# An MLP up-projection as seven half-size products for each pair of weight tiles, with the weight sums on GpSimd and the down-projection interleaved

## The chip, the cores and the metric

The kernel runs on one core of a Trainium2 chip. TensorE (PE in the profile) multiplies matrices into PSUM, VectorE (DVE), ScalarE (ACT) and GpSimd (POOL) work elementwise, and SyncE (SP) issues most DMAs. The metric is the device time of one execution in microseconds (us); lower is better.

## The reference, cut to what matters

One layer of a hybrid diffusion block works on 512 latent tokens and 256 context tokens of width 1024. The change touches only its last part, the MLP:

```
def sq_relu_mlp(h, w1, w2):
    a = jax.nn.relu(h @ w1)
    return (a * a) @ w2

x = x + g2 * sq_relu_mlp(modulate(rmsnorm(x, norm2_g), sh2, sc2), mlp_w1, mlp_w2)
return rmsnorm(x, final_g)
```

`h` is 512 x 1024, `w1` is 1024 x 4096, `w2` is 4096 x 1024, all in float32.

## The kernel before

**Precision.** Every float32 operand is split into a high part in the format float32r and a low part (the rest). `split` does this with an ACT cast (L58) and a DVE subtraction (L59). A product is three matmuls, high by high, high by low and low by high (`mm3`, L71 to L73). `weights` fetches a 128 x 1024 weight tile by DMA into the pool `wraw` (2 buffers), and splits it into the pool `wsp` (3 buffers).

**The MLP.** `h` is kept transposed in `h2`. The 4096 hidden columns are 32 weight tiles of 128. `up` makes for each tile 8 x 3 = 24 matmuls of 512 columns into one PSUM bank, then `square_relu` reads the bank and writes a hidden tile `aT` (high and low). After each 8 tiles, `down` takes the 8 hidden tiles of the chunk before through `w2`, in 2 x 4 steps of 24 matmuls of 512 columns (bank tiles `pd`, stationary `aT`, moving weights), and adds the result to `y2` (the tile `acc`).

**The turn into the MLP.** `half1(t)` makes the second half of the output projection for the token tile t (0 to 3) and from it `xn`, the normalized rows; the factor of the norm comes from a small GpSimd power (L93, tile `ss`). `norm2(t, xn)` transposes `xn` on PE and splits it into `h2`. The first three up tiles are made in halves of 256 columns, so that PE can work on the tokens 0 to 255 while the tokens 256 to 511 are still being normalized.

**Order.** A scheduler lays down one order for each engine when the program is built; each engine takes its instructions strictly in that order, and waits at the first that isn't ready. Where a pool has no free buffer, the first writer of the next tile waits for the last reader of the old one.

Of the kernel before, what the change touches and what calls it, by code (L numbers as in the profile page):

```python
# [36 lines left out]
def dit_block(ctx: ExitStack, tc: tile.TileContext, a: dict):  # L37
# [31 lines left out]
    def mm3(out, st, mv, start, stop):

        PE.matmul(out, st[0], mv[0], start=start, stop=False)  # L71
        PE.matmul(out, st[0], mv[1], start=False, stop=False)  # L72
        PE.matmul(out, st[1], mv[0], start=False, stop=stop)  # L73
# [559 lines left out]
    def hidden():
        return zp[len(aTs) % 2].tile([P, 2, 8, SEQ], F32R, tag="aT", name="aT")

    def up_part(pu, w, lo, n):
        for k in range(KD):
            mm3(pu[:, lo:lo + n], [w[:, h, k * P:(k + 1) * P] for h in range(2)],
                [h2[:, h, k, lo:lo + n] for h in range(2)], k == 0, k == KD - 1)

    def square_relu(pu, aT, i):
        r = sgp.tile([P, SEQ], F32, tag="sg", name="r")
        S.activation(r, pu, AF.Relu)  # L643
        V.tensor_tensor(r, r, r, op=ALU.mult)  # L644
        split(aT[:, 0, i, :], aT[:, 1, i, :], r)

    def up(c, aT, i0=0):
        for i in range(i0, 8):
            w = weights(a["w1"][c * 8 + i])
            pu = psZ.tile([P, 512], F32, tag="u", name="pu1")  # L650
            up_part(pu, w, 0, SEQ)
            square_relu(pu, aT, i)

    def down(c, aT):
        for n in range(2):
            sl = slice(n * 512, (n + 1) * 512)
            pd = [psZ.tile([P, 512], F32, tag="d", name="pd") for _ in range(NT)]
            for ii in range(4):
                w = weights(a["w2"][c, n, ii])
                for t in range(NT):  # L660
                    for i2 in range(2):
                        i = 2 * ii + i2
                        mm3(pd[t], [aT[:, h, i, t * P:(t + 1) * P] for h in range(2)],
                            [w[:, h, i2 * 512:(i2 + 1) * 512] for h in range(2)], i == 0, i == 7)
# [22 lines left out]
    aTs = []  # L687
    aTs.append(hidden())
    first = []
    for i in range(3):  # L690
        w = weights(a["w1"][i])
        pu = psZ.tile([P, 512], F32, tag="u", name="pu1")
        first.append((pu, w))
        if i == 0:
            norm2(2, xn2)
        if i == 2:
            norm2(3, xn3)
        up_part(pu, w, 0, 256)
    for i, (pu, w) in enumerate(first):
        up_part(pu, w, 256, 256)  # L700
        square_relu(pu, aTs[0], i)
    go.close()
    zp.append(pool(gz, "zp1", 1, side="right"))
    up(0, aTs[0], 3)
    for c in range(1, 4):
        aTs.append(hidden())
        up(c, aTs[c])
        down(c - 1, aTs[c - 1])
# [126 lines left out]
```

## Time and profile before

| | |
|---|---|
| Time, median of 3 runs | 821.05 us (819.18 to 821.83) |
| The profiled execution's own time | 821.07 us |
| Its span (first to last instruction) | 819.3 us |
| PE, DVE, ACT, POOL busy | 97%, 56%, 38%, 5% of the span |
| Chain of work that ended last | 93% PE |

Busy time counts an instruction from its start to its end. Matmuls overlap in the pipeline, so the rate of PE is read from the distance between starts (the pitch) and not from the duration of one; the same holds, in a smaller measure, for DVE.

### The profile page before, as it was taken

The page shows a single profiled execution, that of the slowest core. Times are in us where ns is not written, and L with a number is a line of the kernel's source. Part 1 is how long each engine was busy: PE and PEld are TensorE (multiplying, and loading weights), DVE is VectorE, ACT ScalarE, POOL GpSimd, SP SyncE. Part 2 cuts the span into 40 slices and gives each one's busy share as a digit, 9 for nine tenths or more (in the row PEclk, how much of TensorE's full clock was granted, in tenths as well). Part 3 has the DMA queues.
Part 4 walks back from the last instruction along what each step waited for, and adds up shares of the span by engine and source line. Part 5 has one row for each costly group of instructions (what it writes and reads, how often), then busy time and mean ns, then how long its engine had stood idle before and what let it go on. Part 6 is the DMA issues. An engine that isn't in the chain of part 4 may idle for free.

```text
span 819.3 us, 10030 instructions
## 1 busy us (share of the span) xinstructions
PE 797.6 (97%) x3944; PEld 659.6 (81%) x3944; DVE 459.8 (56%) x689; ACT 307.6 (38%) x490; POOL 37.8 (5%) x72
## 2 busy tenths in 40 slices
PE   5999998999999999999999999999999999999996
PEld 4779987888877888888888988888888888888885
DVE  4564537797878888434458654442234324433773
ACT  5434436464772322322344244333333222431132
POOL 1000012121210000000000000000000000000001
PEclk9999999999999999999999999999999999999998
DMA  8653232332208887332434032322232233223122
GB/s 331 252 194 106 83 97 62 92 94 78 81 27 313 297 319 251 103 103 97 184 131 154 1 117 90 102 100 82 102 103 83 97 103 102 79 103 103 60 94 103
DMA packets 33522, 103.98 MB, mean 127 GB/s; under 512 B 8002, under 2 KB 8130, under 8 KB 33474
## 3 DMA queue, kind: packets, MB, share of 16 engines
q1 hardware_dynamic: 32834, 100.99, 35.7%
q0 software_dynamic: 640, 2.36, 1.4%
q8 instruction: 31, 0.51, 0.3%
q14 instruction: 17, 0.13, 0.0%
HBM read 98.87 MB, written 2.10 MB: 123 GB/s over the span
## 4 chain that ended last, share of the span: by engine, by line
PE 93%; DVE 3%; ACT 1%; issue 1%; DMA 1%; SPq 0%; POOLq 0%; POOL 0%; DVEq 0%; ACTq 0%
PE pu L73 8%; PE pu L72 8%; PE pu L71 7%; PE pd L71 7%; PE pd L73 7%; PE pd L72 7%; PE pg L73 5%; PE pg L72 5%; PE pg L71 5%; PE pbr L73 2%; PE pbr L72 2%; PE pbr L71 2%; PE vacc L71 2%; PE vacc L72 1%; PE tp L405 1%; PE vacc L73 1%
## 5 line engine op out<-in xcount | busy, mean ns | idle before, releaser
L59 DVE TENSOR_TENSOR w<-raw,w 128x1024 fp32r<-128x1024 f32 x114 | 141.1, 1238 | 132.0 <-ACT w L58 132.0
L58 ACT CAST w<-raw 128x1024 fp32r<-128x1024 f32 x114 | 119.3, 1046 | 158.1 <-PE pd L73 88.3
L73 PE MATMUL pu<-h,w 128*128 128x512 f32 (+1 forms) x280 | 105.6, 377 | 0.0
L72 PE MATMUL pu<-h,w 128*128 128x512 f32 (+1 forms) x280 | 105.4, 376 | 0.0
L71 PE MATMUL pu<-h,w 128*128 128x512 f32 (+1 forms) x280 | 104.0, 371 | 0.0
L71 PE MATMUL pd<-w,aT 128*128 128x512 f32 x224 | 88.0, 393 | 0.0
L73 PE MATMUL pd<-w,aT 128*128 128x512 f32 x224 | 87.6, 391 | 0.0
L72 PE MATMUL pd<-w,aT 128*128 128x512 f32 x224 | 86.9, 388 | 0.0
L73 PE MATMUL pg<-hx,w 128*128 128x512 f32 x192 | 76.4, 398 | 0.0
L72 PE MATMUL pg<-hx,w 128*128 128x512 f32 x192 | 76.2, 397 | 0.0
L71 PE MATMUL pg<-hx,w 128*128 128x512 f32 x192 | 74.9, 390 | 0.0
L644 DVE TENSOR_TENSOR r<-r 128x512 f32<-128x512 f32 x32 | 22.2, 693 | 87.7 <-ACT r L643 87.5
L71 PEld LDWEIGHTS pu<-h,w 128*128 128x128 f32 x280 | 53.6, 191 | 10.1
L72 PEld LDWEIGHTS pu<-h,w 128*128 128x128 f32 x280 | 52.6, 188 | 9.9
L643 ACT ACTIVATE r<-pu 128x512 f32<-128x512 f32 x32 | 19.1, 597 | 109.8 <-PE pu L73 109.8
L73 PEld LDWEIGHTS pu<-h,w 128*128 128x128 f32 x280 | 52.6, 188 | 9.1
L73 PEld LDWEIGHTS pd<-w,aT 128*128 128x128 f32 x224 | 41.9, 187 | 9.9
L72 PEld LDWEIGHTS pd<-w,aT 128*128 128x128 f32 x224 | 42.0, 188 | 9.3
L71 PEld LDWEIGHTS pd<-w,aT 128*128 128x128 f32 x224 | 42.1, 188 | 8.7
L496 DVE SCALAR_TENSOR_TENSOR acc<-ada,sig,acc 128x1024 f32<-128x1024 f32 x32 | 40.9, 1282 | 9.0 <-DMA ada<-in_adaB 8.8
L71 PEld LDWEIGHTS pg<-hx,w 128*128 128x128 f32 x192 | 36.8, 192 | 8.0
L72 PEld LDWEIGHTS pg<-hx,w 128*128 128x128 f32 x192 | 36.1, 188 | 7.9
(258 smaller groups left out, 1445.2 us busy)
## 6 DMA issues: line engine op xcount, KB each, us to landing
raw<-in_w SPq DMA_DIRECT2D x64, 512.0 KB, 3.3
ada<-in_adaB SPq DMA_DIRECT2D x32, 512.0 KB, 4.9
raw<-in_wG SPq DMA_DIRECT2D x24, 512.0 KB, 3.4
raw<-in_adaA SPq DMA_DIRECT2D x16, 512.0 KB, 5.8
raw<-in_wM SPq DMA_DIRECT2D x8, 512.0 KB, 3.3
raw<-in_wO SPq DMA_DIRECT2D x8, 512.0 KB, 3.2
raw<-in_wC SPq DMA_DIRECT2D x6, 512.0 KB, 3.3
q<-q POOLq DMA_DIRECT2D x8, 288.0 KB, 3.1
```

What stands on the lines that cost most here:

```text
L58: S.copy(hi, src)
L59: V.tensor_tensor(lo, src, f(hi), op=ALU.subtract)
L71: PE.matmul(out, st[0], mv[0], start=start, stop=False)
L72: PE.matmul(out, st[0], mv[1], start=False, stop=False)
L73: PE.matmul(out, st[1], mv[0], start=False, stop=stop)
L405: PE.transpose(tp[:, i, :], pr[:, i * P:(i + 1) * P], ident)
L496: V.scalar_tensor_tensor(acc[:, q, :], raw, sigv[:, k, 0:1], acc[:, q, :], op0=ALU.mult, op1=ALU.add)
L643: S.activation(r, pu, AF.Relu)
L644: V.tensor_tensor(r, r, r, op=ALU.mult)
```

## The change

Two hidden tiles form a pair, and the up-projection of a pair is made as a 2 x 2 block product: `h` is cut into four blocks (tokens 0 to 255 and 256 to 511, features 0 to 511 and 512 to 1023), the two weight tiles `ra` and `rb` into their upper and lower 512 features. Strassen's scheme in Winograd's form gives the four blocks of the result with seven products of half-size blocks in place of eight. So a pair takes 7 x 4 x 3 = 84 matmuls of 256 columns in place of 48 of 512.

The blocks of `h` that the products need are `A11`, `A12`, `A22` and four sums (`Sq`), made once in `norm2_first` and `norm2_second`. For the weights of each pair four sums of 512 columns are made on GpSimd (`sums`: `ta` and `tb`). Each pair splits 3.5 tiles (`ra`, `ta`, `tb` and half of `rb`) where it split 2. The results are put together by accumulating in PSUM (bank `A` goes through products 1, 6, 7 and 4) and by copies and adds of 256 columns. Two steps of the down-projection of the chunk before stand inside each pair from pair 4 on. `g1b`, `fgb` and the pools of the stage are placed anew.

```diff
+    A11, A12, A22 = [h2p.tile([P, 2, 4, HT], F32R, name=f"A{q}") for q in ("11", "12", "22")]
...
+    def norm2_first(t, xn):
+        sl = slice(t * P, (t + 1) * P)
+        for g, tp in enumerate(turned(t, xn)):
+            q = (A11, A12)[g]
+            split(q[:, 0, :, sl], q[:, 1, :, sl], tp)
+            (S.copy if g else V.tensor_copy)(Af[:, g, :, sl], tp)
+    def norm2_second(t, xn, Sq):
...
+        a21 = piece("a21")
+        S.copy(a21, t21)
+        s1 = piece("s1")
+        V.tensor_tensor(s1, t22, a21, op=ALU.subtract)
+        keep(0, s1)
+        split(A22[:, 0, :, sl], A22[:, 1, :, sl], t22)
+        s2 = piece("s2")
+        V.scalar_tensor_tensor(s2, s1, -1.0, Af[:, 0, :, sl], op0=ALU.mult, op1=ALU.subtract)
+        keep(1, s2)
+        s3 = piece("s3")
+        V.tensor_tensor(s3, Af[:, 0, :, sl], a21, op=ALU.subtract)
+        keep(2, s3)
+        s4 = piece("s4")
+        V.scalar_tensor_tensor(s4, s2, -1.0, Af[:, 1, :, sl], op0=ALU.mult, op1=ALU.subtract)
+        keep(3, s4)
...
+        def first_weights(self):
+            self.ra = wraw.tile([P, RAW], F32, tag="raw", name="ra")[:, :D]
+            nc.sync.dma_start(self.ra, a["w1"][2 * self.j])
+            self.rb = mx.tile([P, D], F32, tag="rb", name="rb", bufs=2)
+            nc.sync.dma_start(self.rb, a["w1"][2 * self.j + 1])
+            self.w1 = wsp.tile([P, 2, RAW], F32R, tag="w", name="w")
+            split(self.w1[:, 0, :D], self.w1[:, 1, :D], self.ra)
+        def sums(self):
...
+            G.tensor_tensor(ta[:, :512], ra[:, :512], rb[:, :512], op=ALU.add)
+            G.tensor_tensor(ta[:, 512:], ta[:, :512], rb[:, 512:], op=ALU.add)
+            G.tensor_tensor(tb[:, :512], rb[:, :512], rb[:, 512:], op=ALU.add)
+            G.tensor_tensor(tb[:, 512:], ta[:, 512:], ra[:, 512:], op=ALU.add)
...
+            split(self.w2[:, 0, :D], self.w2[:, 1, :D], ta)
+            self.b22 = mx.tile([P, 2, 512], F32R, tag="b22", name="b22")
+            split(self.b22[:, 0], self.b22[:, 1], rb[:, 512:])
...
+        def p7(self):
+            self.product(self.A, self.w3, 0, self.sq(2), False)
+            V.tensor_tensor(self.r[1][:, HT:], self.A[:, :HT], self.a5, op=ALU.add)
+            self.finish(1)
+        def p4(self):
+            self.product(self.A, self.w3, 512, [A22[:, h] for h in range(2)], False)
+            S.copy(self.r[0][:, HT:], self.A[:, :HT])
+            self.finish(0)
...
+    for j, p in enumerate(pairs):
...
+        if j > 1:
+            p.first_weights()
+            p.p1()
+        p.sums()
+        p.p5()
+        if j:
+            pairs[j - 1].p4()
+        if j > 1:
+            p.p2()
+        step(d)
+        p.p6()
+        p.last_sums()
+        p.p3()
+        step(d + 1)
+        p.p7()
+    pairs[15].p4()
```

**What moves on GpSimd, at the turn into the MLP.** These are POOL's instructions there, first of the kernel before: the four powers (`ss`, one for each token tile) stand together.

```order
L490 MEMSET acc 128x4096
L93 TENSOR_TENSOR ss_3555<-ss_3555,mhalf 128x1 x4
L737 TENSOR_TENSOR ss_6036<-ss_6036,mhalf 128x1
```

And of the change (`ta` and `tb` are the weight sums of pair 0, then of pair 1):

```order
L94 TENSOR_TENSOR ss_3559<-ss_3559,mhalf 128x1 x3
L700 TENSOR_TENSOR ta<-ra,rb 128x512
L702 TENSOR_TENSOR tb<-rb 128x512
L701 TENSOR_TENSOR ta<-ta,rb 128x512
L94 TENSOR_TENSOR ss_3559<-ss_3559,mhalf 128x1
L703 TENSOR_TENSOR tb<-ta,ra 128x512
L700 TENSOR_TENSOR ta<-ra,rb 128x512
```

The power of the last token tile now stands behind three weight sums. The first of them needs `rb`, whose buffer lies in memory that `mT` held, so its DMA waits for a matmul six before the end of `half1(3)`.

**What moves on DVE, right behind that power.** In the kernel before, DVE's last rows for the norm are these (xn is the last token tile, h its split; two more h splits follow, and then the hidden tiles begin):

```order
L92 TENSOR_SCALAR ss_3555<-ss_3555 128x1
L59 TENSOR_TENSOR h_3541<-tp_3891,h_3541 128x4x128
L613 SCALAR_TENSOR_TENSOR xn<-xn,ss_3555,b2b 128x512 x2
L59 TENSOR_TENSOR h_3541<-tp_3898,h_3541 128x4x128
```

In the change the last xn is followed by the rest of token tile 2 and then by tile 3 (s_4053 to s_4067 are its four sums, Sq the splits of the sums, w the splits of the weights):

```order
L616 SCALAR_TENSOR_TENSOR xn<-xn,ss_3559,b2b 128x512 x2
L654 SCALAR_TENSOR_TENSOR s_3983<-s_3977,Af 128x512
L733 TENSOR_TENSOR r<-pB,e_4008 128x256
L657 TENSOR_TENSOR s_3987<-Af,a_3975 128x512
L60 TENSOR_TENSOR Sq<-s_3983,Sq 128x4x128
L660 SCALAR_TENSOR_TENSOR s_3991<-s_3983,Af 128x512
L60 TENSOR_TENSOR Sq<-s_3987,Sq 128x4x128
L733 TENSOR_TENSOR r<-pB,e_4039 128x256
L60 TENSOR_TENSOR Sq<-s_3991,Sq 128x4x128
L650 TENSOR_TENSOR s_4053<-tp_4046,a_4051 128x512
L60 TENSOR_TENSOR w<-ta,w 128x1024
L60 TENSOR_TENSOR Sq<-s_4053,Sq 128x4x128
```

So 11 rows stand between the last xn and the first split `Sq` that product 5 needs; another 11 follow up to the split of `tb` of pair 1 (the splits of `A22` and `b22`, three sums, three of their splits, and three weight splits).

**What stands on ACT in a pair with down steps.** In the kernel before a weight split never stands behind a copy that PE has just made possible, except at the four copies of `acc`. In the change (e_5489 and e_5516 are copies of products 1 and 5, r the copy of product 4, the first w behind it the weights of the first down step):

```order
L59 CAST w<-ta 128x1024
L727 COPY e_5489<-pA 128x256
L59 CAST aT<-r 128x512
L739 COPY e_5516<-pC 128x256
L757 COPY r<-pA 128x256
L59 CAST w<-raw 128x1024
```

The cast of the down step's weights stands behind the copy of product 4, and both wait for that product.

## Rows read from the trace of the kernel before

**Rows 1.** The page: busy time of each engine, and the chain's shares.
```profile
PE 797.6 (97%) x3944; PEld 659.6 (81%) x3944; DVE 459.8 (56%) x689; ACT 307.6 (38%) x490; POOL 37.8 (5%) x72
...
PE 93%; DVE 3%; ACT 1%; issue 1%; DMA 1%; SPq 0%; POOLq 0%; POOL 0%; DVEq 0%; ACTq 0%
```

**Rows 2.** Groups by form: up matmuls; count | busy us, mean ns | idle.
```profile
L73 PE MATMUL pu<-h,w 128*128 128x512 f32 x232 | 92.1, 397 | 0.0
...
L71 PE MATMUL pu<-h,w 128*128 128x256 f32 x48 | 13.7, 285 | 0.0
```

**Rows 3.** Timeline of PE, up tiles; start us, duration us, instruction.
```profile
457.46 0.28 PE L72 MATMUL pu<-h,w 128*128 128x256 f32 x1
...
462.94 0.28 PE L73 MATMUL pu<-h,w 128*128 128x256 f32 x1
...
486.70 0.40 PE L72 MATMUL pu<-h,w 128*128 128x512 f32 x1
...
492.25 0.40 PE L72 MATMUL pu<-h,w 128*128 128x512 f32 x1
```

**Rows 4.** Timeline of the turn: VectorE, then GpSimd, then TensorE.
```profile
458.06 0.68 DVE L59 TENSOR_TENSOR h<-tp,h 128x512 fp32r<-128x512 f32 x1
458.66 1.22 DVE L610 TENSOR_TENSOR xn<-x,a2b 128x1024 f32<-128x1024 f32 x1
...
461.27 1.41 DVE L613 SCALAR_TENSOR_TENSOR xn<-xn,ss,b2b 128x512 f32<-128x512 f32 x2 [0.66 <-POOL ss L93]
...
460.68 0.55 POOL L93 TENSOR_TENSOR ss<-ss,mhalf 128x1 f32<-128x1 f32 x1 [5.92 <-DVE ss L92]
...
463.06 1.04 PE L620 MATMUL tp<-ident,xn 128*128 128x128 f32 x8
```

**Rows 5.** Timeline of VectorE: 128x1024 work back to back.
```profile
774.29 1.22 DVE L713 TENSOR_TENSOR acc<-acc,g2b 128x1024 f32<-128x1024 f32 x1
775.42 1.22 DVE L59 TENSOR_TENSOR w<-raw,w 128x1024 fp32r<-128x1024 f32 x1
```

**Rows 6.** Timeline of GpSimd, VectorE: a GpSimd subtraction beside a PSUM read.
```profile
122.29 0.76 POOL L394 TENSOR_TENSOR bj<-cols,bt 128x256 f32<-128x256 f32 x1
122.99 0.30 POOL L400 MEMSET bj<- 128x256 f32 x1
...
122.60 0.68 DVE L295 TENSOR_TENSOR Kst<-pk,Kst 64x512 fp32r<-64x512 f32 x1 [2.39 <-ACT Kst L294]
```

**Rows 7.** Groups of GpSimd: a memset of one column.
```profile
L356 POOL MEMSET z<- 128x1 f32 x2 | 0.2, 94 | 2.7 <-DVE y L363 2.7
```

**Rows 8.** Timelines of VectorE and GpSimd, two places where both read SBUF.
```profile
145.00 1.77 DVE L59 TENSOR_TENSOR w<-raw,w 128x1024 fp32r<-128x1024 f32 x1
...
144.77 0.93 POOL L394 TENSOR_TENSOR bj<-cols,bt 128x256 f32<-128x256 f32 x1 [1.39 <-DVE mx L424]
...
161.24 1.22 DVE L59 TENSOR_TENSOR w<-raw,w 128x1024 fp32r<-128x1024 f32 x1
162.38 1.25 DVE L59 TENSOR_TENSOR cvT<-y,cvT 128x512 fp32r<-128x512 f32 x1
...
161.40 1.68 POOL L394 TENSOR_TENSOR bj<-cols,bt 128x256 f32<-128x256 f32 x1 [2.85 <-DVE mx L424]
```

**Rows 9.** DMA issues: count, size, median us from issue to landing.
```profile
raw<-in_w SPq DMA_DIRECT2D x64, 512.0 KB, 3.3
```

**Rows 10.** Timelines: a weight tile's hand-over in a down step.
```profile
558.26 0.39 PE L73 MATMUL pd<-w,aT 128*128 128x512 f32 x1
...
558.73 1.05 ACT L58 CAST w<-raw 128x1024 fp32r<-128x1024 f32 x1 [4.44 <-PE pd L73]
...
559.82 1.23 DVE L59 TENSOR_TENSOR w<-raw,w 128x1024 fp32r<-128x1024 f32 x1 [4.27 <-ACT w L58]
```

**Rows 11.** Windows: busy us of PE, PEld, DVE, ACT, POOL; PEclk, DMA share, GB/s.
```profile
126.20:129.00 2.80, 0.35 (x3) 0.33 (x3) 2.73 (x5) 1.99 (x3) 0.30 (x1) 0.99 0.21 53
129.00:132.30 3.30, 3.30 (x13) 2.91 (x12) 2.12 (x9) 1.99 (x6) 0.71 (x2) 0.50 0.44 140
```

More of the change, by code (lines that the diff above doesn't have):

```diff
@@ L67, in weights, with mm3 @@
         return w
[L69 to L73, printed above, removed]
+    def mm3(out, st, mv, start, stop, **kw):
+        PE.matmul(out, st[0], mv[0], start=start, stop=False, **kw)
+        PE.matmul(out, st[0], mv[1], start=False, stop=False, **kw)
+        PE.matmul(out, st[1], mv[0], start=False, stop=stop, **kw)
     ident = const.tile([P, P], F32, name="ident")
@@ L530, in dit_block @@
     x2 = x2p.tile([P, NT, D], F32, name="x2")
-    g1b = x2p.tile([P, D], F32, name="g1b")
     g2b = x2p.tile([P, D], F32, name="g2b")
-    fgb = x2p.tile([P, D], F32, name="fgb")
-    nc.sync.dma_start(fgb, a["final_g"].partition_broadcast(P))
     gh2 = ExitStack()
     h2p = pool(gh2, "h2p", 1)
-    h2 = h2p.tile([P, 2, KD, SEQ], F32R, name="h2")
+    A11, A12, A22 = [h2p.tile([P, 2, 4, HT], F32R, name=f"A{q}") for q in ("11", "12", "22")]
     go = ExitStack()
     op_ = pool(go, "op", 1)
+    g1b = op_.tile([P, D], F32, name="g1b")
     a2b = op_.tile([P, D], F32, name="a2b")
     b2b = op_.tile([P, D], F32, name="b2b")
+    Af = op_.tile([P, 2, 4, HT], F32, name="Af")
+    gw = ExitStack()
+    wop = pool(gw, "wop", 4)
     nc.sync.dma_start(a2b, a["norm2_g"].partition_broadcast(P))
@@ L547, in total @@
     def total(q, n):
-        pg = psZ.tile([P, 512], F32, tag="u", name="pg")
+        pg = psZ.tile([P, 512], F32, tag="a", name="pg", bufs=2)
         w = parts[q]
@@ L591, in dit_block @@
         nc.sync.dma_start(raw, a["wO"][1, kk])
-        w = op_.tile([P, 2, D], F32R, tag="wo", name="wo", bufs=4)
+        w = wop.tile([P, 2, D], F32R, tag="wo", name="wo")
         split(w[:, 0], w[:, 1], raw)
@@ L620, in norm2 @@
                 PE.transpose(tp[:, i, :], xn[:, (4 * g + i) * P:(4 * g + i + 1) * P], ident)
-            split(h2[:, 0, 4 * g:4 * g + 4, t * P:(t + 1) * P], h2[:, 1, 4 * g:4 * g + 4, t * P:(t + 1) * P], tp)
+            out.append(tp)
+        return out
+    def norm2_first(t, xn):
[4 more added lines that the diff above has]
+            (S.copy if g else V.tensor_copy)(Af[:, g, :, sl], tp)
@@ new lines, in norm2_second, with piece, keep @@
+    def norm2_second(t, xn, Sq):
+        sl = slice((t - 2) * P, (t - 1) * P)
+        t21, t22 = turned(t, xn)
+        def piece(name):
+            return op_.tile([P, 4, P], F32, tag="tmp", name=name, bufs=3)
+        def keep(i, src):
+            split(Sq[i][:, 0, :, sl], Sq[i][:, 1, :, sl], src)
+        a21 = piece("a21")
[13 more added lines that the diff above has]
+        keep(3, s4)
@@ L623, in dit_block @@
     xn0, xn1 = half1(0), half1(1)
-    xn2 = half1(2, lambda: norm2(0, xn0))
-    xn3 = half1(3, lambda: norm2(1, xn1))
+    xn2 = half1(2, lambda: norm2_first(0, xn0))
+    xn3 = half1(3, lambda: norm2_first(1, xn1))
+    gw.close()
     gm.close()
     gz = ExitStack()
-    zp = [pool(gz, "zp0", 1, side="right")]
+    Sp = pool(gz, "Sp", 1, side="right")
+    Sq = [Sp.tile([P, 2, 4, HT], F32R, tag="S", name="Sq", bufs=4) for _ in range(4)]
+    mx = pool(gz, "mx", 1, side="right")
+    mxe = pool(gz, "mxe", 2, side="right")
@@ L631, in dit_block @@
     y2 = acc
[L633 to L664, printed above, removed]
+    aTs = [[] for _ in range(4)]
@@ new lines, in dit_block, with hid, down_step @@
+    pairs = [Pair(j) for j in range(16)]
+    for p in pairs:
+        p.out = {}
+    def hid(c, i):
+        return pairs[4 * c + i // 2].out[i % 2]
+    pds = {}
+    def down_step(c, n, ii):
+        sl = slice(n * 512, (n + 1) * 512)
+        if ii == 0:
+            pds[n] = [psZ.tile([P, 512], F32, tag="d", name="pd") for _ in range(NT)]
+        pd = pds[n]
+        w = weights(a["w2"][c, n, ii])
+        for t in range(NT):
+            for i2 in range(2):
+                i = 2 * ii + i2
+                mm3(pd[t], [hid(c, i)[:, h, t * P:(t + 1) * P] for h in range(2)],
+                    [w[:, h, i2 * 512:(i2 + 1) * 512] for h in range(2)], i == 0, i == 7)
+        if ii == 3:
@@ L677, in finish @@
         if lo == 0:
-            sss.append(wl.tile([P, 3], F32, tag="ss3", name="ss3"))
+            sss.append(wl.tile([P, 3], F32, tag="ss3", name="ss3", bufs=4))
         i = 0 if lo == 0 else 1 if lo == 512 else 2
@@ L685, in finish, with step @@
             V.tensor_tensor(xs, xs, fgb[:, :n], op=ALU.mult)
[L687 to L701, printed above, removed]
-    go.close()
[L703 to L708, printed above, removed]
+    pairs[0].first_weights()
+    pairs[1].first_weights()
+    norm2_second(2, xn2, Sq)
+    pairs[0].p1()
+    pairs[0].p2()
+    pairs[1].p1()
+    norm2_second(3, xn3, Sq)
+    pairs[1].p2()
+    go.close()
+    zp = pool(gz, "zp", 12, side="right")
+    for j, p in enumerate(pairs):
+        c = j // 4 - 1
+        d = 2 * (j % 4)
+        def step(d):
+            if c >= 0:
+                down_step(c, d // 4, d % 4)
+        if j > 1:
[14 more added lines that the diff above has]
+    pairs[15].p4()
     gh2.close()
-    wl = pool(gl, "wl", 4)
+    wl = pool(gl, "wl", 1)
+    fgb = wl.tile([P, D], F32, name="fgb")
+    nc.sync.dma_start(fgb, a["final_g"].partition_broadcast(P))
     sss = []
@@ L714, in dit_block @@
         V.tensor_tensor(x2[:, t, :], x2[:, t, :], y2[:, t, :], op=ALU.add)
-    down(3, aTs[3])
+    for ii in range(4):
+        down_step(3, 0, ii)
     ws = []
@@ L719, in dit_block @@
         nc.sync.dma_start(raw, a["w2"][3, 1, ii])
-        w = wl.tile([P, 2, D], F32R, tag="wl", name="wl")
+        w = Sp.tile([P, 2, D], F32R, tag="S", name="wl", bufs=4)
         split(w[:, 0], w[:, 1], raw)
@@ L730, in dit_block @@
                 c0 = (i % 2) * 512 + lo
-                mm3(pd, [aTs[3][:, h, i, t * P:(t + 1) * P] for h in range(2)],
+                mm3(pd, [hid(3, i)[:, h, t * P:(t + 1) * P] for h in range(2)],
                     [ws[i // 2][:, h, c0:c0 + n] for h in range(2)], i == 0, i == 7)
```

53 lines of the change are left out of this document (50 added, 3 removed).

## The prediction

> **What bounds the kernel now.** I read the page first: PE is busy for 797.6 us, 97% of the span, and holds 93% of the chain that ended last, with DVE at 56%, ACT at 38% and POOL at 5% [rows 1]. So a matmul saved is time saved, as long as what feeds PE keeps up. Then the groups by form: 3 x 232 = 696 up matmuls of 512 columns and 3 x 48 = 144 of 256 columns [rows 2]. Their means (397 and 285 ns) overlap; the pace is in the starts. Between 457.46 and 462.94 us lie 46 steps, 0.119 us for 256 columns with a new weight load each; between 486.70 and 492.25 lie 24 steps, 0.231 us for 512 columns [rows 3]. Last the turn into the MLP, where PE has the least in hand: the last xn is normalized at 461.27 (two instructions, 1.41 us) just behind POOL's power, and PE takes its transposes at 463.06 without a gap [rows 4].
>
> **What the change removes.** Before: 696 x 0.231 + 144 x 0.119 = 177.9 us. After: 16 pairs x 84 x 0.119 = 159.9 us. PE gets 18.0 us shorter; down and everything ahead keep their matmuls. The clock is at full speed in both. One product is 12 x 0.119 = 1.43 us, a pair 10.0 us, and a pair with two down steps (48 x 0.231) 21.1 us.
>
> **What the new work costs, each.** On DVE, 1024 columns take 1.13 us (774.29 to 775.42 [rows 5]), 512 columns 0.60 (458.06 to 458.66 [rows 4]), an xn instruction of 512 columns 0.67 (1.41 for two, less the overlap of 0.08 that the 0.68 us row shows against its 0.60 pitch); for the new adds of 256 columns I take 0.35, just over half of 0.60. POOL's add of 512 columns isn't in the trace. The nearest row is a subtraction of 256 columns: 0.76 us long, with the next instruction 0.70 behind it [rows 6]. A POOL instruction of one column is 94 ns [rows 7], so 0.1 is fixed and I take 0.1 + 2 x 0.60 = **1.3 us**. Bounds: 1.52 (twice 0.76), and 0.9, which is 0.70 and a second 256 columns at the memset's 0.30 less 0.1.
>
> The Trainium skill's GPSIMD Engine Reference, section 3.1, gives 4497 ns for a float32 add of 2048 columns; a quarter is 1.12 us, an estimate by that page. By it the sum below would be 3 us lower, and its sign the same.
>
> POOL's work isn't free for DVE. At 145.00 a DVE split of two SBUF inputs took 1.77 us instead of 1.22, behind a POOL subtraction that began at 144.77; at 161.40 POOL itself took 1.68 instead of 0.76 beside the split of 161.24, and the DVE split behind it 1.25 instead of 0.68 [rows 8]. So the two take turns. A DVE instruction that reads PSUM isn't touched: 0.68 us at 122.60 inside a POOL subtraction [rows 6]. So each weight sum holds up DVE's two-SBUF-input work by up to its own length.
>
> **The turn, where most of it goes.** (a) The power for the last token tile stands on POOL behind three weight sums of pair 0. The first wants `rb`, whose memory is released six matmuls before 456.47, so at about 455.3; a transfer of this size lands 3.3 us after issue [rows 9], at 458.7. Three sums take 3.9 us, to 462.6, and DVE's two-input work there (x2 0.60, xn 1.13, a sum 0.60) takes turns with them; I count 2.0 of its 2.3, since x2 may come ahead. With its own 0.55 [rows 4] the power ends at about 465.2, against 461.2 now. With the fourth sum pushing in between the two xn instructions (1.3), xn is complete at 465.2 + 1.4 + 1.3 = 467.9, against 462.7 now. Queued behind that wait is all of DVE's work on token tiles 2 and 3.
>
> (b) PE meanwhile has products 1 and 2 of pairs 0 and 1, 48 matmuls: 457.3 to 463. Before, three half up tiles covered this stretch, and h needed nothing but its split. Now product 5 needs the 11 DVE rows listed above behind xn: two three-operand sums at the price of an xn instruction (1.35), six rows of 512 columns (3.6), one of 1024 (1.13), two of 256 (0.7): 6.8 us, to 474.7. Then 11 more up to the split of `tb` of pair 1: two three-operand sums 1.35, three weight splits 3.4, six rows of 512 columns 3.6, together 8.3 us. Product 3 of pair 0 wants the last split of a sum, 6.1 us in; two POOL sums for pair 1 (2.6) fall into this, 1.2 of them beside DVE's two readers of PSUM: 474.7 + 6.1 + 1.4 = 482.2. Behind it come seven products in a row, 10.0 us: pairs 0 and 1 end at 492.4. Without a stall, 13 products and 16 transposes from 457.26 would end at 457.3 + 18.6 + 0.8 = 476.7 (the 0.8 is eight transposes, 463.06 to 463.86, since the first eight lie ahead). So **+15.7**.
>
> (c) After a gap PE has run at half clock here: busy 0.35 of 2.80 us at 126.20 to 129.00, then 3.3 us at a granted clock of 0.50 [rows 11]. That costs half of 3.3 us after the longest wait, **+1.5**, and more if there are several.
>
> (d) Pair 2: DVE is behind. The split of `tb` of pair 1 ends at 474.7 + 8.3, with 1.4 and 2.6 us for four POOL sums, so at 487.0. Behind it stand three adds (1.05), b22 (0.6), four rows on hidden tiles (2.5) and the splits of `ra` and `ta` of pair 2 (2.3), 6.5 us, and two POOL sums: the split of `ta` ends near 496.1. Product 5 of pair 2 wants it at 492.4 + 1.43. **+2.3**.
>
> **The pairs.** (e) Pairs 2 and 3 have no down steps. PE needs 10.0 us; DVE has 3.5 weight splits (4.0), two hidden tiles (2.5), three adds (1.1): 7.6, of which 6.6 reads two SBUF inputs, and POOL 5.2. They take turns: about 12.3 with 0.5 of overlap. 2 x 2.3 = **+4.6**.
>
> (f) The 12 pairs with down steps have 21.1 us for 15 of DVE (7.6 and two down splits) and POOL (5.2), so throughput is no bound, but two hand-overs are tight with three `wsp` buffers. Before, the last matmul on a buffer starts at 558.26 and is through its step at 558.49, ACT's cast of the next tile starts 0.24 later at 558.73 and takes 1.05, DVE's subtraction starts at 559.82 and takes 1.23: 2.6 us in all [rows 10]. In the change the first down step's tile takes the buffer that product 4 frees, its cast stands behind the copy of product 4 (256 columns, about 0.37), and only product 2 (1.43) covers it: 0.24 + 0.37 + 1.05 = 1.66, so 0.2 late. The second step's tile has 21 matmuls of 256 columns (2.5) to cover those 2.6, and up to 1.3 more where a `tb` sum gets in ahead of the split. I take 0.5 a pair: 12 x 0.5 = **+6**, with bounds 0.3 and 1.5.
>
> (g) The tail: DVE's eight 1024-column instructions on `acc` and x2, and four adds, now stand ahead of a weight split that a down step of the last chunk waits for: **+1.4**, the part that a down step (5.5) with two in hand does not cover. `fgb`, loaded late, lies behind the whole last down block, and costs nothing; were it late it would cost 3.3 [rows 9]. SP's queue carries 16 more half-megabyte issues at their old rate, far from its limit.
>
> **Sum.** -18.0 + 15.7 + 1.5 + 2.3 + 4.6 + 6 + 1.4 = +13.5, against the profiled execution's own 821.07 (span 819.3 and 1.8 around it), 0.02 from the median: **834.6 us**.
>
> **The rivals.** *Stalls outweigh the gain, 835* (0.55): rows 4, 6 and 8 speak for it; its own range is 827 to 844: about 17 POOL sums on the path at 0.9 (-7) or 1.5 (+3.5), and half of (f)'s way to its upper bound (+6). *Faster, 815* (0.20): POOL's sums fit between DVE's work and the power isn't late. Then xn ends at 462.7, product 5 can start at 469.7, PE loses 6.7, (f) 3.6 and (g) 1.4: 11.7 of 18.0. It decides as soon as all stalls stay under 18; rows 4 speak against it, since the chain through DVE was already just in time. *No change, 820* (0.10): stalls of 16 to 20, the turn as (b) but pairs as in the fast case. *Much slower, 850* (0.15): the second `tb` sum wins its turn ahead of the split in every pair (+1.0 x 12), and the sums take 1.5. That the smaller products don't pay on PE, because a weight load is as long as a matmul of 256 columns, is excluded by rows 3: they run at 0.119 with a load each.
>
> **How the numbers follow.** 0.3% (2.5 us) is about what a measurement of this kernel can tell from no change. Range: 815 takes in half of the fast case, 850 half of the slow one. Faster 0.20, same 0.10, slower 0.70.
>
> **What would show it.** In the new profile: products at 0.119; PE idle 8 to 12 us ahead of product 5 of pair 0, with DVE waiting on `ss` from POOL until 465; DVE splits of 1.7 us and more beside POOL's sums; a granted clock of half near 470 to 490; short waits on ACT and DVE at down steps. If `ss` is on time, or POOL's sums take under 1 us, I am wrong, towards 815. If PE waits over 1 us in each pair, towards 850.

## The result, and the profile after

The changed kernel takes **830.28 us** (median of four, 829.58 to 831.71) against 821.24 of the kernel before: ratio 1.0117, 95% interval 1.0094 to 1.0140, slower, as forecast. 834.6 was predicted, 4.3 too high; the forecast's own range was 827 to 844. The profiled execution took 830.66 us, its span 828.9.

The page of the changed kernel, its busy time and its chain, against [rows 1]:

```profile
PE 792.3 (96%) x4448; PEld 677.3 (82%) x4448; DVE 538.5 (65%) x785; ACT 343.9 (41%) x564; POOL 139.7 (17%) x136
...
PE 84%; DVE 7%; ACT 3%; issue 3%; POOL 1%; DMA 1%; SPq 0%; POOLq 0%; ACTq 0%; DVEq 0%
```

PE is still busy for 96%, yet 9 points of the chain have left it: work that PE doesn't do, and waits in its place. The windows show where (columns as in [rows 11]); the turn in five pieces, pairs 2 and 3, pair 4, pairs 5 to 15, and the tail up to the last down block:

```profile
457.00:462.50 5.50, 5.40 (x46) 5.19 (x44) 5.46 (x7) 3.22 (x8) 4.13 (x3) 1.00 0.27 110
462.50:472.50 10.00, 3.00 (x13) 2.74 (x13) 9.00 (x15) 5.33 (x9) 3.25 (x3) 0.83 0.16 53
472.50:478.00 5.50, 3.10 (x12) 2.60 (x12) 5.05 (x6) 2.05 (x4) 3.12 (x2) 0.54 0.05 7
478.00:483.50 5.50, 5.42 (x24) 5.13 (x25) 5.47 (x6) 1.77 (x4) 2.30 (x2) 0.53 0.26 92
483.50:494.60 11.10, 9.13 (x75) 8.73 (x74) 8.14 (x10) 5.45 (x9) 8.35 (x5) 1.00 0.29 94
494.60:517.60 23.00, 21.28 (x170) 20.26 (x169) 21.23 (x23) 12.07 (x22) 11.65 (x8) 1.00 0.28 93
517.60:540.40 22.80, 21.84 (x134) 19.26 (x133) 13.62 (x17) 8.10 (x12) 8.12 (x5) 1.00 0.41 138
540.40:774.70 234.30, 234.30 (x1455) 210.19 (x1453) 134.52 (x161) 94.01 (x139) 61.46 (x40) 1.00 0.29 95
774.70:799.70 25.00, 23.73 (x110) 19.37 (x109) 19.02 (x22) 8.44 (x11) 0.00 (x0) 1.00 0.33 106
```

From 462.5 to 478 DVE is busy for 14.05 of 15.5 us and PE for 6.1: the turn belongs to VectorE. At 472.5 to 483.5 the granted clock is 0.54 and 0.53, the lower of its two levels (1.2 of 2.4 GHz), behind a stretch in which PE was busy for 3.00 of 10.00 us. From pair 5 to 15 PE is never seen idle.

For all kernels below I use one length, the **stage**: from the start of the first up matmul to that of the first matmul of the last down block (`wl`). What lies ahead of it differs by up to 1.5 us from run to run, what lies behind it by up to 1.2. Before it is 457.26 to 790.13, 332.9 us; after, 457.03 to 799.70, **342.7 us**. Work without a wait would be 16 pairs of 9.99 us (the pace of pairs 2 and 3 where nothing waits: in no_sums below, pairs 2, 3 and 4 begin at 485.34, 495.33 and 505.32), 672 down matmuls at 0.2305 and eight transposes at 0.1: 315.5. So the change takes 17.3 us of work from PE and puts in 27 us of waiting:

| stretch of PE | predicted | measured |
|---|---|---|
| work removed | -18.0 | -17.3 |
| (b, c) pairs 0 and 1, to 494.58 | 15.7 + 1.5 | 18.2 |
| (d, e) pairs 2 and 3, to 517.64 | 2.3 + 4.6 | 3.1 |
| (f) pair 4, to 540.42, and 5 to 15 | 6 | 1.7 + 2.7 |
| (g) the tail | 1.4 | 1.4 |
| sum | 13.5 | 9.8 |

The pace of the products is as read from [rows 3]: on PE's timeline 24 steps lie between these two starts of the changed kernel, 0.118 us each.

```profile
754.85 0.28 PE L72 MATMUL pC<-Sq,w 128*128 128x256 f32 x1
...
757.69 0.28 PE L72 MATMUL pB<-A,w 128*128 128x256 f32 x1
```

**The turn.** PE's timeline of the changed kernel, the rows with a wait (in brackets: idle time, and what ended it):

```profile
466.45 1.09 PE L624 MATMUL tp<-ident,xn 128*128 128x128 f32 x4 [4.05 <-DVE xn L616]
...
472.55 0.39 PE L72 MATMUL pC<-Sq,w 128*128 128x256 f32 x1 [3.09 <-ACT Sq L59]
473.63 0.58 PE L73 MATMUL pC<-Sq,w 128*128 128x256 f32 x1 [0.70 <-DVE Sq L60]
...
478.05 0.58 PE L72 MATMUL pA<-Sq,w 128*128 128x256 f32 x1 [1.70 <-ACT Sq L59]
...
488.20 0.39 PE L72 MATMUL pA<-A,w 128*128 128x256 f32 x1 [1.08 <-DVE r L752]
...
493.05 0.39 PE L72 MATMUL pA<-Sq,w 128*128 128x256 f32 x1 [0.89 <-ACT e L744]
```

First the transposes wait for the last xn, then product 5 for the sums of h. GpSimd's timeline there:

```profile
458.37 1.67 POOL L700 TENSOR_TENSOR ta<-ra,rb 128x512 f32<-128x512 f32 x1 [4.52 <-DMA rb<-in_w]
460.00 2.28 POOL L702 TENSOR_TENSOR tb<-rb 128x512 f32<-128x512 f32 x1
462.24 1.78 POOL L701 TENSOR_TENSOR ta<-ta,rb 128x512 f32<-128x512 f32 x1
463.98 0.54 POOL L94 TENSOR_TENSOR ss<-ss,mhalf 128x1 f32<-128x1 f32 x1
464.49 1.26 POOL L703 TENSOR_TENSOR tb<-ta,ra 128x512 f32<-128x512 f32 x1
```

and VectorE's, beside it:

```profile
458.92 2.20 DVE L613 TENSOR_TENSOR xn<-x,a2b 128x1024 f32<-128x1024 f32 x1
461.05 1.24 DVE L611 TENSOR_TENSOR ss<-ss 128x1 f32<-128x1 f32 x1
...
464.55 2.41 DVE L616 SCALAR_TENSOR_TENSOR xn<-xn,ss,b2b 128x512 f32<-128x512 f32 x2 [1.00 <-POOL ss L94]
```

The add of one column (`ss`) in power_first below, where no sum runs beside it:

```profile
461.38 0.16 DVE L612 TENSOR_TENSOR ss<-ss 128x1 f32<-128x1 f32 x1
```

Step (a) stands as written: the power ends at 464.52 (465.2 predicted, 461.2 before [rows 4]), xn at 466.96 (467.9). The rows show the two engines taking turns: xn takes 2.20 us instead of 1.22 behind a sum, and the add of one column behind it, which the power waits for, takes 1.24 us instead of 0.16. A sum that meets nothing takes 1.29 us (1.26 here); I had taken 1.3. From the 4497 ns for 2048 columns in the Trainium skill's GPSIMD Engine Reference, section 3.1, the estimate was 1.12 us; the measured 1.29 decides.

What the prediction's step (b) left out is that the chain also runs through the order of work on ScalarE. ScalarE's timeline, and then VectorE's:

```profile
476.43 1.04 ACT L59 CAST w<-ta 128x1024 fp32r<-128x1024 f32 x1 [3.45 <-POOL ta L701]
477.38 0.61 ACT L59 CAST Sq<-s 128x512 fp32r<-128x512 f32 x1
...
485.06 1.05 ACT L59 CAST w<-tb 128x1024 fp32r<-128x1024 f32 x1 [3.03 <-POOL tb L703]
```

```profile
486.14 1.34 DVE L60 TENSOR_TENSOR w<-tb,w 128x1024 fp32r<-128x1024 f32 x1 [2.27 <-ACT w L59]
...
487.74 0.41 DVE L752 TENSOR_TENSOR r<-pA,e 128x256 f32<-128x256 f32 x1
```

PE's wait until 478.05 is for the cast at 477.38. Its sum of h was ready at 475.26, but it stands behind the cast of `ta` of pair 1, which waited for GpSimd. PE's wait until 488.20 is for the add at 487.74, which stands on VectorE behind the split of `tb` of pair 1; that split waited for a cast that again waited for GpSimd.

### The profile page after: what moved, and what is told of

It is laid out like the page before. It is cut to its first block, busy times and chain, and to the rows that moved or that the text cites. A ratio compares the mean times of both kernels' runs of the same rounds, so it can differ in the third digit from the quotient of the medians.

```text
span 828.9 us, 11302 instructions
## 1 busy us (share of the span) xinstructions
PE 792.3 (96%) x4448; PEld 677.3 (82%) x4448; DVE 538.5 (65%) x785; ACT 343.9 (41%) x564; POOL 139.7 (17%) x136
## 4 chain that ended last, share of the span: by engine, by line
PE 84%; DVE 7%; ACT 3%; issue 3%; POOL 1%; DMA 1%; SPq 0%; POOLq 0%; ACTq 0%; DVEq 0%
PE pd L72 7%; PE pd L73 7%; PE pd L74 7%; PE pg L74 5%; PE pg L73 5%; PE pg L72 5%; PE pA L73 3%; PE pA L74 3%; PE pA L72 3%; DVE w L60 2%; PE pbr L73 2%; PE pbr L74 2%; PE pbr L72 2%; PE vacc L72 2%; PE pC L74 1%
## 5 line engine op out<-in xcount | busy, mean ns | idle before, releaser
L60 DVE TENSOR_TENSOR w<-raw,w 128x1024 fp32r<-128x1024 f32 x82 | 102.0, 1244 | 92.8 <-ACT w L59 92.7
L59 ACT CAST w<-raw 128x1024 fp32r<-128x1024 f32 x82 | 86.0, 1048 | 128.0 <-PE pd L74 63.1
L702 POOL TENSOR_TENSOR tb<-rb 128x512 f32<-128x512 f32 x16 | 23.2, 1451 | 171.6 <-DVE w L60 171.6
L497 DVE SCALAR_TENSOR_TENSOR acc<-ada,sig,acc 128x1024 f32<-128x1024 f32 x32 | 41.0, 1282 | 10.3 <-DMA ada<-in_adaB 10.2
L94 POOL TENSOR_TENSOR ss<-ss,mhalf 128x1 f32<-128x1 f32 x10 | 6.6, 657 | 236.7 <-DVE ss L93 236.7
L72 PEld LDWEIGHTS pg<-hx,w 128*128 128x128 f32 x192 | 36.8, 192 | 8.0
L73 PEld LDWEIGHTS pg<-hx,w 128*128 128x128 f32 x192 | 36.1, 188 | 8.0
L74 PEld LDWEIGHTS pg<-hx,w 128*128 128x128 f32 x192 | 36.1, 188 | 7.3
L72 PE MATMUL pA<-Sq,w 128*128 128x256 f32 x128 | 37.4, 293 | 3.4 <-ACT Sq L59 1.7
L510 ACT ACTIVATE sg<-pg 128x512 f32<-128x512 f32 x21 | 12.5, 597 | 61.3 <-PE pg L74 61.3
L59 ACT CAST w<-ta 128x1024 fp32r<-128x1024 f32 x16 | 16.8, 1050 | 51.0 <-PE pd L74 44.3
L72 PE MATMUL pA<-A,w 128*128 128x256 f32 x128 | 36.2, 283 | 1.1 <-DVE r L752 1.1
L60 DVE TENSOR_TENSOR w<-ta,w 128x1024 fp32r<-128x1024 f32 x16 | 22.1, 1381 | 23.2 <-ACT w L59 23.2
```

The costliest lines, as they stand in the source:

```text
L72: PE.matmul(out, st[0], mv[0], start=start, stop=False, **kw)
L73: PE.matmul(out, st[0], mv[1], start=False, stop=False, **kw)
L74: PE.matmul(out, st[1], mv[0], start=False, stop=stop, **kw)
L94: G.tensor_tensor(ss, ss, mhalf[:, 0:n], op=ALU.pow)
L497: V.scalar_tensor_tensor(acc[:, q, :], raw, sigv[:, k, 0:1], acc[:, q, :], op0=ALU.mult, op1=ALU.add)
L510: S.activation(sg, pg, AF.Sigmoid)
```

## The experiments

Each is an edit of the changed kernel, or adds one to an earlier experiment. Ratios are to the kernel before, which ran beside each. The quoted lines are what was expected of a kernel before it ran: a theory with its time, and a rival with its own.

| kernel | median us | ratio, 95% interval | stage us |
|---|---|---|---|
| changed kernel | 830.28 | 1.0117, 1.0094 to 1.0140 | 342.7 |
| no_sums (leaves work out) | 817.01 | 0.9955, 0.9940 to 0.9970 | 328.8 |
| no_h_sums (leaves work out) | 826.56 | 1.0069, 1.0054 to 1.0084 | 337.7 |
| no_sums_at_all (leaves work out) | 810.45 | 0.9868, 0.9851 to 0.9885 | 323.1 |
| power_first | 840.40 | 1.0247, 1.0230 to 1.0264 | 350.8 |
| power_delay | 834.52 | 1.0164, 1.0141 to 1.0186 | 345.3 |
| plain_first | 824.16 | 1.0040, 1.0027 to 1.0054 | 335.3 |
| plain_delay | 820.26 | 0.9989, 0.9971 to 1.0006 | 330.6 |
| sums_on_vector | 822.68 | 1.0023, 1.0009 to 1.0037 | 334.0 |
| plain_vector | 816.59 | 0.9949, 0.9933 to 0.9966 | 327.0 |
| tail_split | 831.55 | 1.0121, 1.0108 to 1.0135 | 341.9 |
| plain_vector_tail | 814.86 | 0.9916, 0.9902 to 0.9929 | 326.4 |
| own_ra | 811.47 | 0.9884, 0.9866 to 0.9902 | 322.6 |

**Whose wait is it? no_sums, no_h_sums, no_sums_at_all.**

```diff
-            ta = mx.tile([P, D], F32, tag="ta", name="ta")
-            tb = mx.tile([P, D], F32, tag="tb", name="tb")
-            G.tensor_tensor(ta[:, :512], ra[:, :512], rb[:, :512], op=ALU.add)
...
+            ta, tb = ra, rb
```

> Leaves out the four weight sums of each pair: ra and rb are split in the places of ta and tb, so GpSimd has nothing to do in the MLP, and the output is not the reference's; TensorE, VectorE's and ScalarE's instructions stay. Measured so far 830.3 us; TensorE waits 26.6 us in the MLP, 18.1 of it up to the end of pair 1. Theory D (the wait at the turn is VectorE's own chain of 22 rows, which the late power and GpSimd's turns only lengthen): xn complete at 462.9 instead of 467.0 (-4.1), no turns in the chain (-4), pairs 2 to 4 freed of most of their 4.6 (-3): 819 us (817 to 822), with 9 to 11 us of waiting left at the turn. Rival P (GpSimd makes nearly all of it): the turn runs through, 808 to 811 us.

```diff
-        V.tensor_tensor(s1, t22, a21, op=ALU.subtract)
-        keep(0, s1)
...
+        keep(0, t21)
...
+        keep(1, t22)
+        keep(2, t21)
+        keep(3, t22)
```

> Leaves out the four sums of each of the token tiles 2 and 3 (the splits Sq read the transposes directly), so the output is not the reference's; eight VectorE rows of 0.60 to 0.67 us, 5.1 us, leave the chain at the turn, and the waits of ScalarE's casts on them. Power, weight sums and all matmuls stay. Theory D: the chain is VectorE's, so the time falls by about its share, 825 us (823.5 to 827). Rival P: the chain waits for GpSimd, 829 to 830.5.

Both edits together, no_sums_at_all:

> Leaves out the weight sums and the sums of h together (ra, rb and the transposes are split in their places), so the output is not the reference's; matmuls stay. In no_sums TensorE still waits 8.7 us longer than its work at the turn. Theory D (that rest is VectorE's chain): eight rows, 5.1 us, leave it: 812 us (811 to 813.5). Rival B (the rest is the missing matmuls and buffers, whoever feeds them): 816 to 817.

The stage falls by 13.9, 5.0 and 19.6 us. The windows of no_sums, same borders as above:

```profile
457.00:494.60 37.60, 31.71 (x250) 31.02 (x249) 33.61 (x53) 23.82 (x42) 0.55 (x1) 0.91 0.20 68
494.60:517.60 23.00, 23.00 (x171) 21.78 (x170) 15.23 (x22) 10.62 (x19) 0.00 (x0) 1.00 0.35 122
```

Without GpSimd's sums nothing waits any more from pair 2 to pair 4, and the turn costs 8.9 us instead of 18.2; without the sums of h as well it costs 3.2. So of the 18.2 at the turn GpSimd's sums make 9.3, and VectorE's eight rows 5.7 of the rest (5.1 worked out); where GpSimd's sums stay, as in no_h_sums, those rows make 4.0 of the turn and 1.1 of pairs 2 and 3. Theory D holds, at the edge: 817.01 and 8.9 lie at the low end of its 817 to 822 and 9 to 11, 826.56 lies inside its range, 810.45 half a microsecond below. GpSimd's share is half of the wait, more than the "only lengthen" of the theory. Rival P, that it makes nearly all, falls. no_sums takes away the late power, the turns and the waits for the sums themselves at once; how the 9.3 splits among them isn't shown.

**Does the late power decide? power_first, power_delay.**

```diff
+        if t == NT - 1:
+            G.tensor_tensor(flag, ss, mhalf[:, 0:1], op=ALU.add)
...
+            if self.j == 0:
+                G.tensor_tensor(ta[:, 0:1], flag, mhalf[:, 0:1], op=ALU.add)
+                G.tensor_tensor(tb[:, 0:1], flag, mhalf[:, 0:1], op=ALU.add)
```

> The power of the last token tile is put ahead of the weight sums of pair 0 on GpSimd by a copy of its result that the sums wait for. Theory D: xn is complete near 463 instead of 467.0 (-4), but the four sums then fall among the 11 rows ahead of product 5 and hold them up by 2 to 4 us: 828 us (826 to 830). Rival P': the late power is what the turn waits for, and the sums have room behind it: 825 to 826.5.

Neither came: 10 us slower. xn is complete at 464.3, as meant, though the stage starts 1.3 us later in this run, but pairs 0 and 1 end 0.8 us later in the stage than without the edit. The sums now fall behind the power, and this is what they hold up on ScalarE and VectorE (timelines of power_first):

```profile
468.96 1.04 ACT L59 CAST w<-ta 128x1024 fp32r<-128x1024 f32 x1 [5.70 <-POOL ta L707]
469.91 0.61 ACT L59 CAST Sq<-s 128x512 fp32r<-128x512 f32 x1
```

```profile
470.55 0.69 DVE L60 TENSOR_TENSOR Sq<-s,Sq 128x512 fp32r<-128x512 f32 x1 [3.97 <-ACT Sq L59]
```

ScalarE takes its instructions in order: the cast of `ta` waits 5.7 us for GpSimd, the cast of a sum of h that was ready stands behind it, and VectorE waits 3.97 us for that. What the power gained was lost one queue further on; my expectation had not followed ScalarE's queue. Another 6 us lie far away, in five pairs with down steps (a further 1.2 us, about 0.14 in each pair with down steps, I can't place). In the changed kernel (GpSimd and VectorE's timelines at the second down step of pair 4):

```profile
532.33 2.34 POOL L703 TENSOR_TENSOR tb<-ta,ra 128x512 f32<-128x512 f32 x1
...
532.29 1.23 DVE L60 TENSOR_TENSOR w<-raw,w 128x1024 fp32r<-128x1024 f32 x1 [4.02 <-ACT w L59]
```

and in power_first, with the matmul that waits for it:

```profile
534.49 1.29 POOL L709 TENSOR_TENSOR tb<-ta,ra 128x512 f32<-128x512 f32 x1
...
534.51 2.35 DVE L60 TENSOR_TENSOR w<-raw,w 128x1024 fp32r<-128x1024 f32 x1 [4.09 <-ACT w L59]
...
536.92 0.50 PE L73 MATMUL pd<-w,aT 128*128 128x512 f32 x1 [0.81 <-DVE w L60]
```

Whoever starts first keeps the other out for its whole length. In the changed kernel VectorE is first by 0.04 to 0.20 us in all of the eleven pairs 4 to 14; in power_first GpSimd is first by 0.02 to 0.03 in five of them, at 1.2 us each. The Trainium skill states the same rule (SBUF — State Buffer, Who interferes with whom): for an instruction with two SBUF inputs against a GpSimd instruction that reads SBUF, the order of issue decides who is blocked. To test it, GpSimd's last sum is put off:

```diff
+            G.memset(tb[:, 512:768], 0.0)
             G.tensor_tensor(tb[:, 512:], ta[:, 512:], ra[:, 512:], op=ALU.add)
```

> power_first with one more GpSimd instruction, a memset of 256 columns (about 0.25 us) that the last sum of tb then overwrites. In power_first five pairs with down steps wait 1.2 us each where GpSimd's last sum starts 0.02 us ahead of VectorE's split of the second down weights; in the changed kernel VectorE starts 0.04 us ahead and no pair waits. Theory T (a tie for the shared turn, decided by hundredths of a microsecond): a later sum loses the tie in every pair, 5 x 1.2 = 6 us come back, 834.5 us (833 to 836). Rival O (the waits come from another order of work, the tie is chance): 839 to 842.

834.52 us, as theory T has it: one more instruction on GpSimd makes the kernel 5.9 us faster (medians; 5.5 by the stage). VectorE is now first by 0.23 us or more in all eleven, and the five pairs that took 22.4 to 24.1 us take 21.4 to 22.9. Rival O falls. These 1.2 us a pair are what step (f) allowed ("up to 1.3") where a `tb` sum gets in ahead of the split, and about what the "much slower" rival of the prediction took for every pair: power_first has them in five.

**Can the turn be covered? plain_first, plain_delay.** Four ordinary tiles first in halves of 256 columns, and the sums of h (`rest`) behind them; the power stays ahead of the weight sums, as in power_first:

```diff
+        split(A21[:, 0, :, sl], A21[:, 1, :, sl], t21)
         split(A22[:, 0, :, sl], A22[:, 1, :, sl], t22)
...
-    pairs[0].p1()
-    pairs[0].p2()
...
+        up_part(pu, w, 0)
+    for pu, w in first:
+        up_part(pu, w, 1)
...
+    for rest in rests:
+        rest()
```

> The first four weight tiles (pairs 0 and 1) are made as ordinary up tiles in halves of 256 columns, with A21 split for them, and the sums of h behind them; pairs 2 to 15 by seven products as before; the power ahead of the weight sums. TensorE gets 2 x (96 - 84) x 0.119 = 2.9 us longer. Theory D: the wait at the turn (18.1) goes, since the sums of h now have 20 us of matmuls over them: 815 us (813 to 818), faster than the kernel before the change. Rival S (the seven products starve wherever they begin, for weights, buffers and turns): the wait comes back ahead of pair 2, 823 to 828.

> plain_first with the same memset ahead of the last sum of tb. In plain_first the eleven stretches from pair to pair with down steps are together 6.4 us longer than 21.27 us each. Theory T: they come back, 818 us (817 to 820), faster than the kernel before. Rival O: 823 to 825.

plain_first came out in rival S's range (824.16), but not by its cause. The turn is gone: pair 2 starts 24.8 us into the stage, with 1.1 us of waiting, and pair 4 at 503.73 instead of 517.64, so the wait doesn't come back ahead of pair 2. What theory D left out lies in the pairs with down steps: from pair 4 to pair 14 nine of eleven take 21.5 to 23.5 us, 8.6 us over eleven times 21.27 (my 6.4 had miscounted), where the changed kernel is 1.8 over. In pairs 4, 5 and 7 GpSimd's last sum is first by 0.02 to 0.03 us, as in power_first. In pairs 12 and 13 PE waits for the same split, but it is the second sum of `ta` that holds it up, late because the first waited for `ra` to land (GpSimd and VectorE in pair 12):

```profile
691.53 1.29 POOL L712 TENSOR_TENSOR ta<-ra,rb 128x512 f32<-128x512 f32 x1 [1.21 <-DMA ra<-in_w]
692.90 1.30 POOL L713 TENSOR_TENSOR ta<-ta,rb 128x512 f32<-128x512 f32 x1
...
693.03 2.25 DVE L60 TENSOR_TENSOR w<-raw,w 128x1024 fp32r<-128x1024 f32 x1 [4.08 <-ACT w L59]
```

With the memset 4.7 us of the stage come back, 3.9 by the medians: 820.26, just above theory T's range, and no difference from the kernel before that can be told. VectorE is first at the last sum in all eleven pairs, so the 4.3 that stay are not that tie; 1.2 of them lie in pair 4 and 0.7 in pair 13, where GpSimd waits for `ra` again. The late `ra` comes back in own_ra.

**Without GpSimd: sums_on_vector, plain_vector.** `G.tensor_tensor` becomes `V.tensor_tensor` in `sums`.

> The weight sums are made on VectorE (2.4 us more a pair), GpSimd has only the powers. Theory D: no turns are taken any more and the power is on time (-4), pairs with down steps take 21.3 us with VectorE at 12 of 21; but the sums of pairs 0 and 1 (4.8 us) join the chain at the turn, and pairs 2 and 3 have 10.0 us of VectorE for 10.0 us of TensorE: 825 us (822 to 828). Rival P: GpSimd makes the loss, so without it 817 as in no_sums.

> Pairs 0 and 1 ordinary as in plain_first, and the weight sums of pairs 2 to 15 on VectorE. Theory D with T: no wait at the turn, no ties; 12 pairs at 21.3, some 2 us of waiting at pairs 2 and 3, 1.7 at the tail: 814 us (812 to 817), faster than both kernels. Rival V (VectorE is now the bound of the pairs): over 820.

sums_on_vector: pairs 2 and 3 take 10.1 us, those with steps 21.3, and the turn still waits 13.9 us, with GpSimd out of it: 5.0 more than in no_sums, where eight sums at 0.60 on VectorE make 4.8. 822.7 is theory D's side (its 825 was 2 high). plain_vector beats both kernels, 816.6 us, 2.6 over my figure: four pairs wait again, up to 1.1 us, now without any GpSimd work. The late `ra` below is why.

**The tail: tail_split, plain_vector_tail.** Step (g) as its rows show it in the changed kernel, PE and then VectorE:

```profile
784.00 0.50 PE L73 MATMUL pd<-w,aT 128*128 128x512 f32 x1 [1.27 <-DVE w L60]
```

```profile
781.59 1.22 DVE L848 TENSOR_TENSOR acc<-acc,g2b 128x1024 f32<-128x1024 f32 x1
782.72 1.22 DVE L60 TENSOR_TENSOR w<-raw,w 128x1024 fp32r<-128x1024 f32 x1
```

```diff
+        if c == 2 and n == 0 and ii == 3:
+            scaled(0)
...
+            V.tensor_tensor(tmp, pd, y2[:, t, lo:lo + n], op=ALU.add)
+            V.tensor_tensor(tmp, tmp, g2b[:, lo:lo + n], op=ALU.mult)
...
-    for t in range(NT):
-        V.tensor_tensor(y2[:, t, :], y2[:, t, :], g2b, op=ALU.mult)
-        V.tensor_tensor(x2[:, t, :], x2[:, t, :], y2[:, t, :], op=ALU.add)
```

> The changed kernel with the work on acc taken from ahead of the last weight splits: the half n=0 is scaled and added when its chunk is done, the half n=1 is added to the last bank tiles in finish (one more VectorE instruction for each, 0.35 us on the end). Theory G (the 1.7 us wait of the second down step of the last chunk is for a weight split behind VectorE's rows on acc): -1.6 + 0.35, 829 us (828.3 to 829.8). Rival: it waits for a transfer or a buffer, 830 to 831.

> plain_vector (816.6 us) with the edit of tail_split: 815.3 us (814 to 817), the fastest of all that compute everything.

In tail_split that wait is gone from the trace: the 90 matmuls ahead of `wl` run without a gap, and the split starts at 781.23, though the last product 7 ahead of it starts 2.0 us later than in the changed kernel. Theory G is right on the place. But the edit gives it back: 0.7 us from the start of `wl` to the end, where two instructions stand for one, and 0.6 in pair 14, where the half n=0 now stands, so the stage is only 0.8 shorter and the median, 831.55, shows no gain: it lies above the ranges of both theory and rival. plain_vector_tail comes to 814.86, as expected, but only 0.6 of the 1.7 us that it gains by the medians are in the stage.

**The late `ra`: own_ra.** In plain_vector_tail, VectorE and then PE at the longest of the waits that plain_vector also had:

```profile
664.41 0.69 DVE L706 TENSOR_TENSOR ta<-ra,rb 128x512 f32<-128x512 f32 x1 [2.72 <-DMA ra<-in_w]
...
666.47 1.22 DVE L60 TENSOR_TENSOR w<-raw,w 128x1024 fp32r<-128x1024 f32 x1
```

```profile
667.75 0.50 PE L73 MATMUL pd<-w,aT 128*128 128x512 f32 x1 [1.16 <-DVE w L60]
```

`ra` was issued at 658.93 only, when its `wraw` buffer came free, and took 5.5 us against a median of 3.2; VectorE waits for it with the weight split behind.

```diff
-            self.ra = wraw.tile([P, RAW], F32, tag="raw", name="ra")[:, :D]
+            self.ra = mx.tile([P, D], F32, tag="ra", name="ra")
-    zp = pool(gz, "zp", 12, side="right")
+    zp = pool(gz, "zp", 11, side="right")
```

> plain_vector_tail (814.9 us) with a buffer of its own for ra, so that ra can be fetched most of a pair earlier and not only when the down weights of the pair before are split; the room is one of the twelve hidden-tile buffers. In plain_vector_tail five pairs with down steps are 0.3 to 1.4 us longer than 21.28, 3.8 us in all, where a first sum waits on VectorE for ra to land and the split of the second down weights stands behind it. Theory R (the late ra is what these pairs wait for): 811 us (810 to 812.5). Rival Z (eleven hidden-tile buffers bring a wait of their own, or the pairs wait for something else): 814 to 817.

811.47 us: theory R, to half a microsecond. In plain_vector_tail VectorE waits for `ra` eleven times, 13.3 us in all; in own_ra it never does, and the pairs that were long take 21.29. The edit also leaves both `wraw` buffers to the down weights; the two effects aren't separated. Its windows show PE without a gap from 480 to 757 us, at full clock:

```profile
457.00:480.00 23.00, 22.81 (x194) 22.60 (x193) 22.45 (x37) 14.74 (x25) 0.93 (x1) 1.00 0.22 83
480.00:500.00 20.00, 20.00 (x169) 19.88 (x168) 19.88 (x31) 12.93 (x21) 0.00 (x0) 1.00 0.29 107
500.00:757.00 257.00, 257.00 (x1594) 230.41 (x1593) 167.54 (x228) 102.00 (x151) 0.00 (x0) 1.00 0.28 95
```

own_ra is 1.2% faster than the kernel before the change (ratio 0.9866 to 0.9902): of the 17.3 us that the seven products save in sixteen pairs, it keeps 10.3 with fourteen.

## Why the prediction was right, and where it was off

The sign and the place were right; of the 4.3 us by which the forecast was too high, 3.7 are in the stage: (d), (e) and (f) were 5.4 too high together, the work removed and the turn 1.7 too low.

- **Work removed, 18.0.** 17.3. The pace and the counts were right.
- **(a), (b) the turn.** Right in the main and nearly in size: product 5 forecast for 474.7, begun at 472.55 and running from 473.63; product 3 of pair 0 for 482.2, begun at 481.4 and running from 483.5; end of pair 1 at 492.4 + 1.5, 494.58. That VectorE's rows and GpSimd's sums make it is shown by the three kernels that leave one or both out (15.0 of 18.2), and by sums_on_vector. What (b) lacked is the order on ScalarE, and it took seven products in a row behind product 3, where PE waited twice (1.08 and 0.89). Ahead of product 5 PE was idle for 7.1 us (4.05 and 3.09), where 8 to 12 was forecast. Its 492.4 is also a slip: 482.2 and 10.0 make 492.2.
- **(c) the clock, 1.5.** Under-sized: 33 matmuls ran at about 0.21 instead of 0.119, 3.1 us, not all of it on the path, since product 6 waited for VectorE in between anyway. How much of the 18.2 it makes wasn't measured by itself.
- **(d) pair 2, 2.3.** Wrong: the split of `ta` ended at 496.37 (496.1 predicted), but pair 2 began 2.2 us later than this step had it (it left out the 1.5 of (c)), so product 5 lost only 0.3. The same delay was counted twice.
- **(e) pairs 2 and 3, 4.6.** Over-sized: 2.8 (3.1 less the 0.3 of (d)). I let every sum hold VectorE up nearly in full; VectorE's rows in these two pairs add up to 22.7 us against 17.9 in no_sums, 4.8 more for eight sums of 1.29.
- **(f) 0.5 a pair.** Over-sized from pair 5 on: 0.25, of it some 0.2 the late cast that was worked out (1.66 against 1.43; PE's weight loads wait for it, in the row below: us in all, times, longest). The 0.3 more for the second step was a tie that this kernel wins and power_first and plain_first lose in part. Pair 4's 1.7 is another wait, ahead of its down steps: products 1 and 5 wait for weight splits.

```profile
PEld pd L72 <- ACT w L59: 2.1, 11, 0.2
```

- **(g) the tail, 1.4.** Right. What the prediction says beside it of SP's queue is wrong: there are no 16 more issues, both kernels fetch 64 tiles of `in_w` (64 before; 32, 16 and 16 for `raw`, `ra` and `rb` after). The sum put nothing on them.
- **The fast rival** needed GpSimd's sums to cost nothing: no_sums shows what that is worth, 13.9 us of the stage and 817 us, close to its 815.

## What to carry to other kernels

Before saving matmuls on a PE-bound kernel, find the place where PE has the least in hand, and count what the new operands cost the engines that feed it there: here a saving of 17 us spread over 320 was lost again in the first 38. Keep the old form for the first tiles, so that the new operands are made under it. And GpSimd was no spare engine beside a VectorE that is on the path: with the ordinary tiles first, moving the sums to VectorE brought 824.16 down to 816.59, and with the sums on GpSimd who was first by 0.02 us set 1.2 us in a pair. Last, read the order on every engine that the chain passes: a wait is handed on to work that was ready behind it.
